# Seven block products in place of eight in parts of eight weight units of a decoder layer

## The chip, the cores and the metric

The kernel runs on one core of one Trainium2 chip. The metric is the device time of one execution in microseconds (us). The core has five engines that work in parallel, each through its own instructions in order: PE (TensorE, matrix products into the PSUM banks), DVE (VectorE), ACT (ScalarE), POOL (GpSimd) and SP (SyncE), which here only issues DMA transfers. POOL issues transfers too.

## The reference

One layer of a decoder trunk on 256 rows of 4096 columns, in float32:

```
u = RMSNorm(h)
one combined projection of u -> branch A (gated recurrence), branch B (differential attention),
                                two sigmoid gates of 4096 columns each
h = h + (sigmoid(g_A) * y_A + sigmoid(g_B) * y_B) @ wo      (y_A, y_B: the branches' outputs, projected)
out = RMSNorm(h)
```

The units that the change touches are plain products with large weights: the gates (u of 256 x 4096 by 4096 x 8192), and the output product (256 x 4096 by 4096 x 4096). The two branch projections (2048 x 4096 each) stand between them.

## The kernel before

**Weights.** All weights stream through one ring. SP loads pieces of 128 x 2048 float32 (1 MB, L104) into three buffers `w`. Each piece is split in two chunks of 1024 columns: ACT writes `hi` (L122), a copy rounded to the matrix engine's float32 format, and DVE writes `lo` = w - hi (L123). `hi` and `lo` have four buffers each, and the split runs up to three chunks ahead of PE (SPLIT_AHEAD). The activations are split in the same way into tiles `u`, `oh` and `y`, with a high and a low part.

**Products.** A product of one 128 x 128 block of activations with 512 columns of weights is three matmuls (L254, L255, L256): high by hi, high by lo, low by hi. One matmul takes 512 columns and accumulates in a PSUM bank of 128 x 512.

**Units.** After eight groups of branch work come eight gate units (`gate_unit`, `wide_unit`), each over 16 pieces: 1024 output columns as two blocks n by the 256 rows as two blocks t, so four banks. One piece holds two k-tiles (blocks of 128 of the inner dimension) by 1024 columns: eight block products, 24 matmuls. In the last piece the four banks are finished one after the other, ACT takes the sigmoid of each out of the bank with the rows' scale `rstd` (L310), and POOL stores it in DRAM (`g_dram`, L311). During gates 1 to 7 SP loads the branch outputs (`ol`), and ACT and DVE split them into `oh`. Then four branch units, each of two `wide_unit`s; DVE multiplies the banks with the gates read back (`gl`, L682, L686) and adds them (L687), PE transposes the result, and ACT and DVE split it into `y` (L696 and after). Last come eight output units of 512 columns (`mov_unit`, 8 pieces each): DVE adds x (`xr`, loaded through POOL) to the bank (L727), ACT squares with a running sum (L728), POOL multiplies with the norm's weight (L729). The last of them keeps six half-pieces (two of them in tiles of their own, `khi` and `klo`), so that the first 128 rows end early and their scaling and stores (`out_rows`, from L731) run beside the rest.

**Order.** The program is written out in Python in order of pieces (`run`); a scheduler turns it into one list per engine, in which loads and splits come before other work of the same time (priority AHEAD). Small work beside the stream is queued in `todo`, one entry after each piece. What an engine does in which order is then fixed.

Of the kernel before, what the change touches and what calls it, by code (L numbers as in the profile page):

```python
# [9 lines left out]
F32 = mybir.dt.float32  # L10
# [29 lines left out]
KEEP = 10  # L40
# [4 lines left out]
def trunk_kernel(ctx, tc, xT, x, nw, w_stat, w_mov, w_gate, w_branch, w_out, lbt, hnw, lamv, slw, fw, out):  # L45
# [8 lines left out]
    gp = ctx.enter_context(tc.tile_pool(name="gp", bufs=4))  # L54
    acc = ctx.enter_context(tc.tile_pool(name="acc", bufs=4, space=PSUM))
    mx = ctx.enter_context(tc.tile_pool(name="mx", bufs=4, space=PSUM))
# [26 lines left out]
    class Stream:  # L83
        def __init__(self):
            self.src = []
            self.raw = {}
            self.split = {}
            self.keep = {}
            self.loaded = 0
            self.done = 0  # L90

# [13 lines left out]

        def split_to(self, n):
            while self.done < min(n, 2 * len(self.src)):
                i = self.done
                self.load_to(i // 2 + 1)
                t = self.raw[i // 2]  # L110
                if i % 2:
                    del self.raw[i // 2]
                t = t[:, (i % 2) * HALF : (i % 2 + 1) * HALF]
                if i in self.keep:
                    hi, lo = self.keep.pop(i)
                else:
                    hi = whi.tile([P, HALF], F32R, name="hi", tag="hi")
                    lo = wlo.tile([P, HALF], F32R, name="lo", tag="lo")
                m = HALF // 2 if i < HEAD else HALF
                with tc.high_priority(AHEAD):  # L120
                    for c in range(0, HALF, m):
                        act.activation(hi[:, c : c + m], t[:, c : c + m], AF.Copy)  # L122
                        dve.tensor_tensor(lo[:, c : c + m], t[:, c : c + m], f32(hi[:, c : c + m]), op=ALU.subtract)  # L123
                self.split[i] = (hi, lo)
                self.done += 1

        def take(self, i):
            self.split_to(2 * i + SPLIT_AHEAD)
            yield self.split.pop(2 * i)
            self.split_to(2 * i + 1 + SPLIT_AHEAD)  # L130
            yield self.split.pop(2 * i + 1)
# [67 lines left out]
    def add(srcs, fn):  # L199

        for n, s in enumerate(srcs):
            stream.src.append(s)
            plan.append((n, fn))

    def run():
        for i in range(run.at, len(plan)):
            n, fn = plan[i]
            stream.load_to(i + LOAD_AHEAD)
            for r, (hi, lo) in enumerate(stream.take(i)):
                fn(2 * n + r, hi, lo)  # L210
            step()
        run.at = len(plan)
# [62 lines left out]
    def wide_unit(srcs, src_tiles, done):  # L275


        st = {}
        last = 2 * len(srcs) - 1

        def cols(r, n):
            c = n if r % 2 else 1 - n
            return slice(c * 512, (c + 1) * 512)

        def fn(r, hi, lo):
            if r == 0:
                st["ps"] = [[acc.tile([P, 512], F32, name="ps_w", tag="acc") for _ in range(2)] for _ in range(2)]
            ps = st["ps"]
            if r < last - 1:
                for n in range(2):  # L290
                    c = cols(r, n)
                    mov_mm([ps[t][n] for t in range(2)], src_tiles[r // 4], r % 4, hi[:, c], lo[:, c], r == 0, False)
                return
            st[r] = hi, lo
            if r < last:
                return
            for n in range(2):
                for t in range(2):
                    for k in (last - 1, last):
                        hi, lo = st[k]  # L300
                        c = cols(k, n)
                        mov_mm({t: ps[t][n]}, src_tiles[k // 4], k % 4, hi[:, c], lo[:, c], False, k == last, (t,))
                    done(t, n, ps[t][n])

        add(srcs, fn)

    def gate_unit(q):
        def done(t, n, ps):
            g = gp.tile([P, 512], F32, name="gt", tag="gt")
            act.activation(g, ps, AF.Sigmoid, scale=rstd[:, t : t + 1])  # L310
            pool.dma_start(g_dram[2 * q + n][t], g)  # L311

        wide_unit([w_gate[q, n] for n in range(16)], u, done)
# [39 lines left out]
    with tc.tile_pool(name="tmp", bufs=1) as tmp:  # L353
# [289 lines left out]
        gate_unit(0)  # L643
        run()
        while todo:
            step()

    with tc.tile_pool(name="op", bufs=1) as op:
        oh = [op.tile([P, 4, 2, S], F32R, name=f"oh{g}") for g in range(8)]

        def o_load(g, a):
            t = op.tile([P, 2, S], F32, name="ol", tag="gl", bufs=4)
            nc.sync.dma_start(t, o_dram[g][:, 2 * a : 2 * a + 2])
            return t

        def o_split(g, a, t):
            c = slice(2 * a, 2 * a + 2)
            act.activation(oh[g][:, c, 0, :], t, AF.Copy)
            dve.tensor_tensor(oh[g][:, c, 1, :], t, f32(oh[g][:, c, 0, :]), op=ALU.subtract)

        ol = {}
        for g in range(8):
            for a in range(2):
                todo.extend([lambda i=(g, a): ol.update({i: o_load(*i)}), None, None, lambda i=(g, a): o_split(*i, ol.pop(i))])
        for q in range(1, 8):
            gate_unit(q)


        y = []

        def branch_unit(q):
            rows, g = {}, {}

            def g_load(br):
                for n in range(2):
                    for t in range(2):
                        gl = g[t, n] = op.tile([P, 512], F32, name="gl", tag="gl", bufs=4)
                        nc.sync.dma_start(gl, g_dram[8 * br + 2 * q + n][t])

            def a_done(t, n, ps):  # L680
                r = rows[t, n] = gp.tile([P, 512], F32, name="yr", tag="gt")
                dve.tensor_tensor(r, ps, g[t, n], op=ALU.mult)  # L682

            def b_done(t, n, ps):
                r, gl = rows[t, n], g[t, n]
                dve.tensor_tensor(gl, ps, gl, op=ALU.mult)  # L686
                dve.tensor_tensor(r, r, gl, op=ALU.add)  # L687
                todo.append(lambda: turn(t, n))

            def turn(t, n):  # L690
                if t == 0:
                    y.append(uy.tile([P, 4, 2, S], F32R, name="y", tag="uy"))
                yt = y[2 * q + n]
                ps = mx.tile([P, 4, P], F32, name="ps_y", tag="mx")
                for j in range(4):
                    pe.transpose(ps[:, j], rows[t, n][:, j * P : (j + 1) * P], ident)  # L696
                c = slice(t * P, (t + 1) * P)
                act.activation(yt[:, :, 0, c], ps, AF.Copy)
# [156 lines left out]
```

## Time and profile before

| what | value |
|---|---|
| device time, median of 3 runs | 2894.07 us (2893.0 to 2894.49) |
| the profiled execution | 2894.51 us, its span 2892.5 us |
| granted TensorE clock, mean | 0.999 of full speed |
| PE busy | 2878.5 us (100%), 13782 instructions |
| DVE busy | 1478.8 us (51%) |
| ACT busy | 1326.0 us (46%) |
| POOL busy | 97.4 us (3%) |
| moved by DMA | 583.15 MB, 202 GB/s |

The span runs from the first to the last instruction of the profiled execution. The matmuls are pipelined: the duration of one contains part of the next, so that their spacing is read from their starts. Busy shares are averages over stages, and an idle engine that nobody waits for costs nothing.

### The profile page before, as it was taken

What the parts mean: (1) busy time and instruction counts of PE and PEld (TensorE: products, weight loads), DVE (VectorE), ACT (ScalarE), POOL (GpSimd) and SP (SyncE); (2) the same over time, 40 slices, a digit from 0 to 9 for tenths busy, and PEclk for the clock granted to TensorE, in tenths of its full rate; (3) what the DMA queues carried; (4) which work ended last, traced back from release to release, by engine and by line L of the source; (5) the groups of instructions that cost most, each with busy time, mean ns of one, the idle gap of its engine ahead of it and who ended that gap; (6) DMA issues with size and microseconds to landing.
All of it is one profiled execution on the core that took longest, in us unless ns stands there. A gap on an engine that the chain in (4) does not pass through costs nothing.

```text
span 2892.5 us, 33800 instructions
## 1 busy us (share of the span) xinstructions
PE 2878.5 (100%) x13782; PEld 2412.5 (83%) x13782; DVE 1478.8 (51%) x1497; ACT 1326.0 (46%) x1507; POOL 97.4 (3%) x113
## 2 busy tenths in 40 slices
PE   9999999999999999999999999999999999999998
PEld 8888888888888888888888888888888888888886
DVE  6546455454555554545545444444444555554444
ACT  7545454454444444444445434444434443344443
POOL 0000000000000000000000000000000000001010
PEclk9999999999999999999999999999999999999999
DMA  8555555555545555555557555556556556566564
GB/s 334 190 177 195 189 182 181 183 197 189 183 178 187 197 182 190 177 190 193 181 190 276 206 198 207 204 206 212 203 193 222 215 205 219 207 220 220 201 212 173
DMA packets 91804, 583.15 MB, mean 202 GB/s; under 512 B 10992, under 2 KB 11264, under 8 KB 26624
## 3 DMA queue, kind: packets, MB, share of 16 engines
q1 hardware_dynamic: 86112, 562.09, 54.9%
q0 software_dynamic: 5536, 18.89, 1.7%
q8 instruction: 108, 1.77, 0.2%
q14 instruction: 48, 0.39, 0.0%
HBM read 564.17 MB, written 16.78 MB: 201 GB/s over the span
## 4 chain that ended last, share of the span: by engine, by line
PE 95%; issue 3%; DMA 1%; ACT 0%; DVE 0%; SPq 0%; POOL 0%; DVEq 0%; ACTq 0%; POOLq 0%
PE ps_s L183 12%; PE ps_m L254 12%; PE ps_m L255 12%; PE ps_m L256 12%; PE ps_w L254 11%; PE ps_w L255 11%; PE ps_w L256 11%; PE ps_s L184 6%; PE ps_k L183 4%; PE ps_k L184 2%; DMA ol<-o_dram 1%; PE ps_sc L477 0%; PE ps_s L566 0%; PE ps_o L492 0%; PE ps_y L696 0%
## 5 line engine op out<-in xcount | busy, mean ns | idle before, releaser
L123 DVE TENSOR_TENSOR lo<-w,hi 128x1024 fp32r<-128x1024 f32 (+1 forms) x1026 | 1265.0, 1236 | 1345.1 <-ACT hi L122 1344.4
L122 ACT ACTIVATE hi<-w 128x1024 fp32r<-128x1024 f32 (+1 forms) x1026 | 1080.7, 1056 | 1473.4 <-PE ps_w L256 582.1
L183 PE MATMUL ps_s<-u,hi 128*128 128x512 f32 x1536 | 540.2, 396 | 0.0
L184 PE MATMUL ps_s<-u,lo 128*128 128x256 f32 x1536 | 431.7, 281 | 0.0
L254 PE MATMUL ps_m<-hi,u 128*128 128x512 f32 x1024 | 402.1, 393 | 0.0
L255 PE MATMUL ps_w<-lo,u 128*128 128x512 f32 x1024 | 399.0, 390 | 0.8 <-DVE lo L123 0.8
L254 PE MATMUL ps_w<-hi,u 128*128 128x512 f32 x1024 | 399.6, 390 | 0.0
L256 PE MATMUL ps_m<-hi,u 128*128 128x512 f32 x1024 | 398.7, 389 | 0.0
L255 PE MATMUL ps_m<-lo,u 128*128 128x512 f32 x1024 | 398.7, 389 | 0.0
L256 PE MATMUL ps_w<-hi,u 128*128 128x512 f32 x1024 | 398.4, 389 | 0.0
L183 PEld LDWEIGHTS ps_s<-u,hi 128*128 128x128 f32 x1536 | 288.0, 188 | 67.8 <-DVE half L190 0.2
L184 PEld LDWEIGHTS ps_s<-u,lo 128*128 128x128 f32 x1536 | 290.1, 189 | 0.3
L254 PEld LDWEIGHTS ps_w<-hi,u 128*128 128x128 f32 x1024 | 192.2, 188 | 42.7 <-ACT gt L310 2.6
L255 PEld LDWEIGHTS ps_w<-lo,u 128*128 128x128 f32 x1024 | 192.2, 188 | 40.7 <-DVE lo L123 1.1
L256 PEld LDWEIGHTS ps_m<-hi,u 128*128 128x128 f32 x1024 | 192.2, 188 | 40.3
L256 PEld LDWEIGHTS ps_w<-hi,u 128*128 128x128 f32 x1024 | 192.2, 188 | 39.9
L254 PEld LDWEIGHTS ps_m<-hi,u 128*128 128x128 f32 x1024 | 192.3, 188 | 39.5
L255 PEld LDWEIGHTS ps_m<-lo,u 128*128 128x128 f32 x1024 | 192.3, 188 | 39.1
L254 PE MATMUL ps_w<-hi,oh 128*128 128x512 f32 x512 | 200.6, 392 | 0.0
L256 PE MATMUL ps_w<-hi,oh 128*128 128x512 f32 x512 | 199.4, 389 | 0.0
L255 PE MATMUL ps_w<-lo,oh 128*128 128x512 f32 x512 | 199.3, 389 | 0.0
L254 PE MATMUL ps_m<-hi,y 128*128 128x512 f32 x504 | 196.5, 390 | 0.0
(182 smaller groups left out, 2254.9 us busy)
## 6 DMA issues: line engine op xcount, KB each, us to landing
w<-in_w_mov SPq DMA_DIRECT2D x156, 1024.0 KB, 4.8
w<-in_w_gate SPq DMA_DIRECT2D x128, 1024.0 KB, 4.8
w<-in_w_stat SPq DMA_DIRECT2D x96, 1024.0 KB, 4.8
w<-in_w_branch SPq DMA_DIRECT2D x64, 1024.0 KB, 4.8
w<-in_w_out SPq DMA_DIRECT2D x64, 1024.0 KB, 4.8
g_dram<-gt POOLq DMA_DIRECT2D x32, 256.0 KB, 5.9
gl<-g_dram SPq DMA_DIRECT2D x32, 256.0 KB, 4.5
o_dram<-oT POOLq DMA_DIRECT2D x8, 512.0 KB, 6.9
```

Source lines behind the costliest of these rows:

```text
L122: act.activation(hi[:, c : c + m], t[:, c : c + m], AF.Copy)
L123: dve.tensor_tensor(lo[:, c : c + m], t[:, c : c + m], f32(hi[:, c : c + m]), op=ALU.subtract)
L183: pe.matmul(ps, wh, ut[:, k].rearrange("p a s -> p (a s)"), start=first, stop=False)
L184: pe.matmul(ps[:, :S], wl, ut[:, k, 0, :], start=False, stop=last)
L254: pe.matmul(ps[t], uh, wh, start=first, stop=False)
L255: pe.matmul(ps[t], uh, wl, start=False, stop=False)
L256: pe.matmul(ps[t], ul, wh, start=False, stop=last)
```

## The change

A piece holds a 2 x 2 block matrix of weights (two k-tiles by two blocks of 512 columns), and the rows and k-tiles of the activations make a 2 x 2 block matrix too. Their product is eight block products as written, and seven by Strassen's method (in Winograd's form), with sums of blocks formed before and after. In five gate units (2 to 6) eight of the 16 pieces, and in three of four output units seven of 16, are now computed by the seven products ("S"); the other pieces stay as they are ("P"), and S and P alternate. Around this:

- For an S piece DVE forms three sums of weight blocks (L132 to L134; one in place, two blocks and one more in a tile `wt` with one buffer), and ACT and DVE split 3.5 chunks instead of 2 (four entries in the stream). `hi` and `lo` now have seven buffers each from gate 1 on, and the split runs up to five chunks ahead.
- The sums of activation blocks (`sf`, four blocks of 128 x 128 per piece) are formed once: for u during gate 1, for y during branch 3 and output unit 0. Before that u is multiplied with `rstd` in place during gate 0 (`norm`), so that the sigmoid needs no scale.
- A mixed unit has eight banks: four products of sums (P1, p5, P6, P7) and four blocks. At its end they are combined (`evict`): two ACT copies, four DVE operations, and one DVE addition per block (L423 in the gate units, L960 in the output units) ahead of the sigmoid or the addition of x. The two PSUM pools of before are closed after gate 0, and one pool of eight named banks takes their place.
- The output units are now four of 1024 columns (the weights are laid out accordingly), the last one with its last three pieces held. h goes to DRAM through POOL and comes back before the end; the multiplication with the norm's weight moves from POOL to DVE. `xr` is loaded by SP, half of the rows at a time. y goes through DRAM as well, stored and loaded through POOL. The loads and splits of the branch outputs move to gate 7.

```diff
+        def sums(self, i):
+            w = self.raw[i]
+            t = self.raw[i, "T"] = self.tp.tile([P, 1536], F32, name="wt", tag="wt")
+            dve.tensor_tensor(w[:, 0:512], w[:, 0:512], w[:, 512:1024], op=ALU.add)
+            dve.tensor_tensor(t[:, 0:512], w[:, 0:512], w[:, 1536:2048], op=ALU.subtract)
+            dve.tensor_tensor(
+                t[:, 512:1536].rearrange("p (a c) -> p a c", a=2), w[:, 512:1536].rearrange("p (a c) -> p a c", a=2),
+                t[:, 0:512].unsqueeze(1).to_broadcast([P, 2, 512]), op=ALU.subtract,
+            )
...
+                    if self.kind[i] == "S" and c == 0:
+                        self.sums(i)
+                    t = self.raw[i] if c < 2 else self.raw[i, "T"]
+                    o = (c % 2) * HALF
+                    w = HALF if c < 3 else 512
...
+    ORDER = (("P1", "p5"), (0, 1), ("P6", "P7"), (2,))
...
+        def evict(b):
+            if b in (0, 1, 2, 3):
+                final(b // 2, b % 2, ps[b], sb.get(("c", b)))
+                return
+            t = sb[b] = gp.tile([P, 512], F32, name="ut", tag="gt")
+            if b == "P1":
+                act.activation(t, ps[b], AF.Copy)
+                sb["c", 0] = t
+            elif b == "p5":
+                act.activation(t, ps[b], AF.Copy)
+            elif b == "P6":
+                dve.tensor_tensor(t, ps[b], sb["P1"], op=ALU.add)
+            else:
+                dve.tensor_tensor(t, ps[b], sb["P6"], op=ALU.add)
+                sb["c", 2] = t
+                dve.tensor_tensor(sb["P6"], sb["p5"], sb["P6"], op=ALU.subtract)
+                sb["c", 1] = sb["P6"]
+                dve.tensor_tensor(sb["p5"], sb["p5"], t, op=ALU.subtract)
+                sb["c", 3] = sb["p5"]
...
+            else:
+                dve.tensor_tensor(g, ps, g, op=ALU.add)
+                act.activation(g, g, AF.Sigmoid)
             pool.dma_start(g_dram[2 * q + n][t], g)
...
+        def norm(n):
+            f = joined(n)
+            dve.tensor_tensor(f, f, rstd_bc.unsqueeze(1).to_broadcast([P, 2, S]), op=ALU.mult)
+            p_form(u[n // 2], 2 * (n % 2), f)
...
+    early.close()
...
+    whi2 = ctx.enter_context(tc.tile_pool(name="whi2", bufs=3))
+    wlo2 = ctx.enter_context(tc.tile_pool(name="wlo2", bufs=3))
...
+    stream.ring = [(whi, wlo)] * 4 + [(whi2, wlo2)] * 3
+    stream.ahead = 5
...
+    SPLIT = (0, 2, 4, 6, 8, 10, 12, 14)
...
+    gate_unit(1, PLAIN, None, bank, post=u_sums)
+    for q in range(2, 7):
+        gate_unit(q, mix(16, SPLIT), us, bank)
+    gate_unit(7, PLAIN, None, bank, post=o_next)
...
+    def y_load(n):
+        t = yl[n] = gp.tile([P, 2, S], F32, name="yl", tag="gt")
+        pool.dma_start(t, y_dram[n // 2][:, 2 * (n % 2) : 2 * (n % 2) + 2])
...
+            else:
+                dve.tensor_tensor(tile_, ps, tile_, op=ALU.add)
+                dve.tensor_tensor(tile_, tile_, xt, op=ALU.add)
+            act.activation(xt, tile_, AF.Square, accum_out=ssq[:, t, b : b + 1])
+            dve.tensor_tensor(tile_, tile_, fwt[n], op=ALU.mult)
...
+            if t == 0 and n == 1:
+                io_x(1)
```

Three places in the order of the instructions. The first is DVE within a gate unit of before; each row is one split, and the numbers tell the buffers apart:

```order
L123 TENSOR_TENSOR lo_12109<-w_12072,hi_12108 128x1024
L123 TENSOR_TENSOR lo_12125<-w_12072,hi_12124 128x1024
L123 TENSOR_TENSOR lo_12143<-w_12106,hi_12142 128x1024
L123 TENSOR_TENSOR lo_12159<-w_12106,hi_12158 128x1024
L123 TENSOR_TENSOR lo_12179<-w_12140,hi_12178 128x1024
```

And DVE within a mixed gate unit now (L153 is the split):

```order
L132 TENSOR_TENSOR w_13119<-w_13119 128x512
L153 TENSOR_TENSOR lo_13122<-w_13085,hi_13121 128x1024
L133 TENSOR_TENSOR wt_13143<-w_13119 128x512
L134 TENSOR_TENSOR wt_13143<-w_13119,wt_13143 128x1024
L153 TENSOR_TENSOR lo_13132<-w_13085,hi_13131 128x1024
L153 TENSOR_TENSOR lo_13142<-w_13119,hi_13141 128x1024
L153 TENSOR_TENSOR lo_13156<-w_13119,hi_13155 128x1024
L153 TENSOR_TENSOR lo_13165<-wt_13143,hi_13164 128x1024
L153 TENSOR_TENSOR lo_13181<-wt_13143,hi_13180 128x512
L132 TENSOR_TENSOR w_13196<-w_13196 128x512
```

A pair of pieces was four splits; it is now six splits and three sums, and both splits of the P piece (`w_13085`) stand behind the first sum of the S piece that follows it (`w_13119`), the second one behind all three sums.

The second place is DVE at the end of a mixed gate unit; before, no DVE work of the unit's end stood there, only splits as above. `ut` are the products of sums, `ps_w` the banks:

```order
L369 TENSOR_TENSOR ut_13233<-ps_w_12683,ut_13205 128x512
L153 TENSOR_TENSOR lo_13252<-wt_13224,hi_13251 128x1024
L371 TENSOR_TENSOR ut_13238<-ps_w_12687,ut_13233 128x512
L153 TENSOR_TENSOR lo_13256<-wt_13224,hi_13255 128x512
L373 TENSOR_TENSOR ut_13233<-ut_13210,ut_13233 128x512
L423 TENSOR_TENSOR ut_13205<-ps_w_12667,ut_13205 128x512
L375 TENSOR_TENSOR ut_13210<-ut_13210,ut_13238 128x512
L423 TENSOR_TENSOR ut_13233<-ps_w_12671,ut_13233 128x512
L423 TENSOR_TENSOR ut_13238<-ps_w_12695,ut_13238 128x512
L423 TENSOR_TENSOR ut_13210<-ps_w_12714,ut_13210 128x512
L153 TENSOR_TENSOR lo_13298<-w_13249,hi_13297 128x1024
L153 TENSOR_TENSOR lo_13310<-w_13249,hi_13309 128x1024
```

The splits of the next unit's first piece (`wt_13224`) stand ahead of the final additions, those of its second piece (`w_13249`) behind all four.

The third place is SP at the end of a mixed output unit; before, SP had only weight loads there (x went through POOL):

```order
L104 DMA w_18769<-in_w_out 128x2048
L104 DMA w_18803<-in_w_out 128x2048
L104 DMA w_18837<-in_w_out 128x2048
L104 DMA w_18871<-in_w_out 128x2048
L104 DMA w_18911<-in_w_out 128x2048
```

Now, with the two loads of x for the ending unit and the two for the next one's first rows:

```order
L120 DMA w_20382<-in_w_out 128x2048
L951 DMA xr_20306<-in_x 128x512
L951 DMA xr_20308<-in_x 128x512
L951 DMA xr_20772<-in_x 128x512
L951 DMA xr_20774<-in_x 128x512
L120 DMA w_20417<-in_w_out 128x2048
```

Four loads of x stand between two weight loads, and SP takes them in this order.

## Rows read from the trace of the kernel before

**Rows 1.** Page: busy us (share) and instructions; clock; chain; costliest DVE group (us, mean ns):

```profile
PE 2878.5 (100%) x13782; PEld 2412.5 (83%) x13782; DVE 1478.8 (51%) x1497; ACT 1326.0 (46%) x1507; POOL 97.4 (3%) x113
PEclk9999999999999999999999999999999999999999
PE 95%; issue 3%; DMA 1%; ACT 0%; DVE 0%; SPq 0%; POOL 0%; DVEq 0%; ACTq 0%; POOLq 0%
L123 DVE TENSOR_TENSOR lo<-w,hi 128x1024 fp32r<-128x1024 f32 (+1 forms) x1026 | 1265.0, 1236 | 1345.1 <-ACT hi L122 1344.4
```

**Rows 2.** Time line inside a gate unit: start, duration, engine, line [idle before <-releaser]:

```profile
1501.18 1.06 ACT L122 ACTIVATE hi<-w 128x1024 fp32r<-128x1024 f32 x1 [1.66 <-PE ps_w L256]
1501.20 0.39 PE L255 MATMUL ps_w<-lo,u 128*128 128x512 f32 x1
...
1501.43 0.39 PE L256 MATMUL ps_w<-hi,u 128*128 128x512 f32 x1
...
1502.27 1.23 DVE L123 TENSOR_TENSOR lo<-w,hi 128x1024 fp32r<-128x1024 f32 x1 [1.49 <-ACT hi L122]
...
1503.90 1.06 ACT L122 ACTIVATE hi<-w 128x1024 fp32r<-128x1024 f32 x1 [1.66 <-PE ps_w L256]
```

**Rows 3.** Window of a gate unit: engines' busy us (instructions), clock, DMA share, GB/s:

```profile
1650.00:1735.00 85.00, 85.00 (x375) 70.11 (x374) 37.93 (x32) 34.72 (x34) 2.16 (x4) 1.00 0.58 205
```

**Rows 4.** Waits of the whole span: us in total, times, longest us:

```profile
DVE lo L123 <- ACT hi L122: 1344.4, 920, 3.5
ACT hi L122 <- PE ps_w L256: 582.1, 346, 3.7
...
PEld ps_w L254 <- ACT gt L310: 3.0, 8, 0.4
...
PE ps_w L255 <- DVE lo L123: 0.8, 1, 0.8
```

**Rows 5.** Time line of POOL: the first store of two gate units that follow each other:

```profile
1650.04 0.54 POOL L311 DMA_DIRECT2D g_dram<-gt  x1 [81.45 <-ACT gt L310]
...
1737.35 0.54 POOL L311 DMA_DIRECT2D g_dram<-gt  x1 [81.47 <-ACT gt L310]
```

**Rows 6.** Time line of DVE with queued work; last, a group (busy, mean ns | idle before):

```profile
2177.34 2.36 DVE L123 TENSOR_TENSOR lo<-w,hi 128x1024 fp32r<-128x1024 f32 x2 [3.53 <-ACT hi L122]
...
2261.06 1.28 DVE L686 TENSOR_TENSOR gl<-ps_w,gl 128x512 f32<-128x512 f32 x2
2262.26 1.28 DVE L687 TENSOR_TENSOR yr<-yr,gl 128x512 f32<-128x512 f32 x2
...
L686 DVE TENSOR_TENSOR gl<-ps_w,gl 128x512 f32<-128x512 f32 x16 | 10.6, 685 | 0.5
```

**Rows 7.** DMA issues; landings of L104 in 1560:2200, in 5:60; GB/s slices of 2150:2200:

```profile
w<-in_w_gate SPq DMA_DIRECT2D x128, 1024.0 KB, 4.8
g_dram<-gt POOLq DMA_DIRECT2D x32, 256.0 KB, 5.9
...
DMA to landing us min/median/max: 4.6/4.8/7.8
...
DMA to landing us min/median/max: 5.2/8.4/9.8
...
GB/s 275 0 118 321 400 13 52 236 439 111 0 144 419 275 0 98 347 393 0 52 111 341 318 370 410 210 311 295 170 262 419 98 13 131 419 288 0 105 315 413
```

**Rows 8.** Time line of the end, from the last bank to the scaling of the rows:

```profile
2881.73 0.69 DVE L727 TENSOR_TENSOR hbuf<-ps_m,xr 128x512 f32<-128x512 f32 x1 [3.12 <-PE ps_m L256]
2882.46 0.63 ACT L728 ACTIVATE xr<-hbuf 128x512 f32<-128x512 f32 x1 [3.90 <-DVE hbuf L727]
...
2883.74 1.76 ACT L739 ACTIVATE hbuf<-hbuf,r_h 128x512 f32<-128x512 f32 x2 [0.23 <-DVE r_h L734]
```

**Rows 9.** Time line of PE in the last output unit, matmuls on the kept tiles:

```profile
2873.24 0.40 PE L254 MATMUL ps_m<-khi,y 128*128 128x512 f32 x1
2873.48 0.40 PE L255 MATMUL ps_m<-klo,y 128*128 128x512 f32 x1
```

More of the change, by code (lines that the diff above doesn't have):

```diff
@@ L39 @@
 HEAD = 4
-KEEP = 10
 AHEAD = 100
@@ L104, in load_part, with tiles @@
             nc.sync.dma_start(self.raw[i][:, c : c + n], self.src[i][:, c : c + n])
-        def split_to(self, n):
[L107 to L119, printed above, removed]
-                with tc.high_priority(AHEAD):
[L121 to L124, printed above, removed]
+        def tiles(self):
+            a, b = self.ring[self.at % len(self.ring)]
+            self.at += 1
+            hi = a.tile([P, HALF], F32R, name="hi", tag="hi")
+            lo = b.tile([P, HALF], F32R, name="lo", tag="lo")
+            return hi, lo
@@ L125, in split_to @@
                 self.done += 1
         def take(self, i):
[L128 to L131, printed above, removed]
+            for n in range(self.first[i], self.first[i] + (4 if self.kind[i] == "S" else 2)):
+                self.split_to(n + self.ahead)
+                yield self.split.pop(n)
     stream = Stream()
@@ L273, in mov_unit @@
         add(srcs, fn)
[L275 to L283, printed above, removed]
-        def fn(r, hi, lo):
[L286 to L292, printed above, removed]
+    ORDER = (("P1", "p5"), (0, 1), ("P6", "P7"), (2,))
@@ L293, in fn @@
                 return
-            st[r] = hi, lo
-            if r < last:
+            if n <= last - tail:
+                plain(n, c, hi, lo, [(0, 0), (0, 1), (1, 0), (1, 1)])
                 return
[L297 to L310, printed above, removed]
-            pool.dma_start(g_dram[2 * q + n][t], g)
-        wide_unit([w_gate[q, n] for n in range(16)], u, done)
+            held[r] = hi, lo
+            if n < last or c == 0:
+                return
+            for blocks in ([[(t, m)] for t in range(2) for m in range(2)] if tail == 1
+                           else [[(t, m) for m in range(2)] for t in range(2)]):
+                for (k, c2), w in held.items():
+                    plain(k, c2, *w, blocks)
@@ L646, in trunk_kernel @@
             step()
[L648 to L698, printed above, removed]
-                dve.tensor_tensor(yt[:, :, 1, c], ps, f32(yt[:, :, 0, c]), op=ALU.subtract)
-            todo.extend([lambda: g_load(0)] + [None] * 7 + [lambda: g_load(1)])
-            wide_unit([w_branch[0, q, n] for n in range(8)], oh[:4], a_done)
-            wide_unit([w_branch[1, q, n] for n in range(8)], oh[4:], b_done)
-        for q in range(4):
-            run()
-            branch_unit(q)
-        run()
@@ L797 @@
+    for q in range(4):
+        out_unit(q)
+    run()
 _OUT = (S, D)
```

346 lines of the change are left out of this document (266 added, 80 removed).

## The prediction

> **What bounds the kernel now.** I read the page first. TensorE (PE) is busy for 100% of the span, its clock stands at the upper of its two levels (2.4 GHz) in every slice, and the chain that ended last is 95% PE [rows 1]. A busy PE need not be PE at its peak, so next comes the time line inside a gate unit: from one matmul to the next of the same form is 0.227 us (1501.20 to 1501.43), although one is listed as 0.39 long, because they overlap. In the 2.72 us between two `hi` copies (1501.18 to 1503.90) lie twelve matmuls, all that one chunk of weights feeds; in the same stretch DVE works once for 1.23 us and idles 1.49, and ACT works 1.06 and idles 1.66 [rows 2]. The windows say the same of a whole unit: 375 matmuls in 85 us, or 0.2267 each, with DVE busy 37.93 and ACT 34.72 [rows 3]. Last the waits: DVE waits 1344 us for ACT, ACT 582 for PE (a chunk buffer to come free), but PE waits for a split once, for 0.8 us. The only other repeated stall of PE is at the start of a gate unit, 8 times up to 0.4 us [rows 4]. So PE's count of matmuls is the time, and a removed matmul is worth 0.2267 us as long as the splits, the weight loads and the evictions keep ahead.
>
> **What is removed.** Each of the 5 mixed gate units turns 8 pieces of 24 matmuls into 8 of 21, each of the 3 mixed output units 7: 61 pieces by 3 matmuls, 183 in all, every one 128x512. 183 x 0.2267 = **41.5 us**, all on the path. The period of a gate unit is 87.3 us (1650.04 to 1737.35) [rows 5]; it should become 87.3 - 24 x 0.2267 = 81.9. The stalls at unit starts mostly go, since a mixed unit opens with banks that were emptied long before: five to six of 0.38 us. With that and the few matmuls on kept halves that go: -1 us or a little more, I take **-1**.
>
> **What is added on DVE.** A Strassen piece (S) has three sums (L132 and L133 of 512 columns, L134 of 1024) and four splits (three of 1024, one of 512), where a plain piece (P) has two splits. One 128x1024 operation is listed as 1236 ns and one 128x512 as 685 [rows 1, 6], but queued operations overlap: two splits took 2.36 together, and two 512-wide products that began at 2261.06 made way for the next at 2262.26, 0.60 each [rows 6]. So 1.13 to 1.24 and 0.60 to 0.69. S costs 4 x 1.13 + 3 x 0.60 = 6.3 (long form 4 x 1.24 + 3 x 0.69 = 7.0), P 2.3 (2.5), a pair 8.6 (9.5). PE needs 24 + 21 = 45 matmuls x 0.2267 = 10.2 for the pair. A mixed gate unit adds 8 evictions on DVE, 4.8 us: 8 x 8.6 + 4.8 = 73.6 of 81.6 (90%); in the long form 81.5, 100%. I take the overlapped form, as DVE's queue will be full; the other end, 100%, costs no more than a few tenths per unit. ACT copies 5.5 chunks per pair, about 1.06 each, 5.8 of 10.2: covered.
>
> **What DVE's order adds.** DVE works strictly in order, and in the mixed units a weight load hangs in that order too. The load of S piece k+1 needs the buffer of the P piece before, whose last reader is the split after L134; that comes 4.8 us after L132 of piece k (0.60 + 1.13 + 0.60 + 1.13 + 1.13, and about 0.2 because L133 and L134 depend on each other). Then 0.3 to issue and 4.8 to land [rows 7] until L132 of piece k+1 may start. The loop is 9.9 us per pair against PE's 10.2: PE stays the bound, by 0.3. Would two loads in flight lengthen the landing? The load of the following P goes out some 2.3 us later, and in a busy slice the DMA engines move up to 439 GB/s, so that a megabyte flows for about 2.4 us of its 4.8 [rows 7]: the flows hardly meet. I take 4.8. The bounds are 4.6 and the 8.4 of the opening, where loads were queued on one another [rows 7]. Break-even is a lasting 5.1 us. The seven split buffers hold about 7.5 us of lead, so that one late load costs nothing.
>
> **Unit ends.** At the end of a mixed unit DVE must stand before the last four additions (L423, L960) until PE has closed the banks, and behind them are queued the splits of the next unit's second piece. The first piece is split already: 21 matmuls, 4.8 us, and the P piece's matmuls begin only after them. In a gate unit the P splits are finished with some 2.9 us to spare by the durations above. In an output unit x must be reloaded for the second half of the rows (two loads behind an ACT square, 4.8 us by the landings of [rows 7]), the additions L961 wait for it, a split waits behind them, and SP holds further x loads ahead of a weight load. There I count a spare of 0.65 to 1 us, so 0 to 3 us of PE idle at each of two such ends. Gate 0 hands over to gate 1 through a closing of the PSUM pools: PE waits for the last sigmoid, **+0.7** (0.69 by the 512-wide DVE row in [rows 6] as the nearest, nothing hides it). In gate 7, SP's loads of `ol` wait for a g_dram write (5.9 us [rows 7]) ahead of a weight load, 0 to 3. For all of these together I take **+2** with 0 to 9 as bounds.
>
> **The tail.** Before, the last bank is followed by an addition at 2881.73 (0.69), a square (0.63) and short steps to the scaling at 2883.74 [rows 8]. Now the last unit ends with two banks per half, so one more addition L960, L961 and multiplication by fw on DVE in that chain, and a small reduction: 2 to 4 steps of 0.60, some of them under the square. **+2.2**, bounds 1 to 4.
>
> **The sum** is made against the profiled execution, 2894.5 us (span 2892.5 and 2.0 around it), 0.4 over the median: 2894.5 - 41.5 - 1 + 0.7 + 2 + 2.2 = 2856.9, by the median 2856.5. I say **2857**. Bounds of the small terms: 2852 to 2866.
>
> A page's price for the removed matmul: the Trainium skill, "TensorE: Matmul & The Clock Gate", section "Wait — 56ns, not 53.3ns?", gives a start-to-start of columns by 2.4 GHz and 2.5 ns, 215.7 ns for 512 columns. The trace shows 227 [rows 2], so by the page the removed term would be 39.5 in place of 41.5; the measurement decides.
>
> **Rivals.** (a) *The loop of sums, splits and loads becomes the bound in part.* For: its 9.9 lies 3% under PE's 10.2, and every duration in it is a median of an uncrowded DVE and of loads that flew alone. Against: two loads hardly meet. At a lasting landing of 5.5 us the pair takes 10.6; 0.4 x 61 = 24 less some 10 that the lead of eight units absorbs, so 2857 + 14 = 2871; at 5.75, 2880. (b) *Slower than before: the same loop, altogether the bound.* One mechanism: the load of an S piece lands so late that L132 holds DVE, and the P splits behind it. It wipes out the gain at a pair of 10.88 us, the 48 matmuls of before, which is a landing of 5.8; at 6.5 a pair takes 11.6: 2857 + 61 x 1.4 - 10 = 2932, 2910 if half of the pairs are hit. For it speaks the opening, 8.4 us with loads queued on one another; against it 4.8 as the median at DMA busy 58% [rows 3, 7], to which the change adds a sixteenth. (c) *Matmuls from other buffers run slower.* The rows on the separately placed `khi` and `klo` start 0.235 apart, where those on `hi` and `lo` start 0.227 apart [rows 9]. Three of the seven split buffers are now placed apart. If their share, three sevenths of some 5,600 matmuls, runs at 0.235: 2400 x 0.008 = 19, 2876; if all of them, 2900, no change. Those rows follow upon a change of tile, so they may show a passing state. (d) *The loads and stores on the POOL queue (y, h) come late beside a busy DVE.* Each of 16 y loads holds ACT in order; at 1.5 us each (a DVE operation and a bit) that is up to 24, less the lead: 2870. The issue on POOL takes 0.54 in the gate stores with DVE half busy [rows 3, 5], which says nothing of a full DVE. The Trainium skill, "SBUF — State Buffer", section "SBUF: two separate sides", says that descriptors of such DMAs wait while DVE holds a port that it shares with GpSimd; by that rule the change moves y to the wrong queue, and no row of before shows such a stall. (e) *The change doesn't do what it says.* The instructions of the changed program hold 183 fewer 512-wide matmuls, so no.
>
> **How the numbers follow.** Forecast 0.60 (2852 to 2866); (a) 0.18 (2866 to 2884); (c) 0.07 (2866 to 2900); (d) 0.04; (b) 0.07 (2900 to 2932, of it 0.02 within a hair of no change); other losses, none over 40 us, 0.04. The range holds the forecast and most of (a), (c) and (d): 2850 to 2882, 0.85 by these cases; I leave the rest for what I may have missed. A measurement of this kernel tells a difference of about 0.2% (6 us) from no change: faster 0.90 (all of the forecast, (a) and (d), most of (c) and of the other losses), same 0.04 (from (b) 0.02, from (c) and the others 0.01 each), slower 0.06 (the rest of (b) and of the others).
>
> **What would show it.** Right: 81.9 us between the first gate stores of two mixed units; 0.227 between matmuls everywhere; the chain still PE; DVE busy near 75% over the mixed units with short idle stretches ended by weight loads at L132. Wrong: PE's weight loads waiting for `lo` or `hi` for more than 10 us in sum (a, b); weight landings over 5.1 us in mixed units (a, b); 0.235 in every third matmul group (c); ACT waiting for `yl` (d); PE idle of over 3 us at each output unit's start (unit ends).

## The result and the profile after

The changed kernel takes **2857.44 us** (median of 4 runs, 2854.89 to 2858.94) against 2894.28 for the kernel before on the same chip; the ratio is 0.9872, with a 95% interval of 0.9855 to 0.9889. The forecast was 2857. The profiled execution took 2858.94 us with a span of 2857.2, which is 35.3 less than before. First the page's busy shares, the clock and DVE's costliest group, as in [rows 1]:

```profile
PE 2838.4 (99%) x13599; PEld 2379.8 (83%) x13599; DVE 1818.1 (64%) x2015; ACT 1447.4 (51%) x1692; POOL 97.9 (3%) x136
PEclk9999999999999999999999999999999999999999
L153 DVE TENSOR_TENSOR lo<-w,hi 128x1024 fp32r<-128x1024 f32 (+1 forms) x1028 | 1257.5, 1230 | 952.1 <-ACT hi L152 947.5
```

13782 matmuls have become 13599, 183 fewer. DVE works 339 us more and is still idle for a third of the whole span. The page's chain of waits says nothing here: it was followed back only as far as 2741, some 4% of the span. What sets the pace is read from the gate units. POOL's time line (start, duration, engine, line, [idle before <-releaser]), the first store of mixed units that follow each other, answers to [rows 5]:

```profile
1735.40 0.54 POOL L425 DMA_DIRECT2D g_dram<-ut  x1 [79.08 <-ACT ut L424]
...
1817.00 0.54 POOL L425 DMA_DIRECT2D g_dram<-ut  x1 [77.92 <-ACT ut L424]
...
1898.60 0.54 POOL L425 DMA_DIRECT2D g_dram<-ut  x1 [77.93 <-ACT ut L424]
```

81.60 us from unit to unit, where it was 87.3. That is 360 matmuls by 0.2267 (81.6): PE alone, without any addition. The window of most of one such unit (busy us of PE, PEld, DVE, ACT, POOL with instructions; clock, DMA share, GB/s) answers to [rows 3]:

```profile
1740.00:1816.00 76.00, 76.00 (x337) 62.94 (x336) 70.36 (x74) 45.95 (x49) 0.00 (x0) 1.00 0.64 225
```

DVE is busy for 70.36 of 76 us, 93%. So the change has brought DVE within a few per cent of becoming the bound, and the gain hangs on that margin. DVE's time line over one pair of pieces shows how it is kept:

```profile
1782.63 0.68 DVE L132 TENSOR_TENSOR w<-w 128x512 f32<-128x512 f32 x1
1783.23 1.22 DVE L153 TENSOR_TENSOR lo<-w,hi 128x1024 fp32r<-128x1024 f32 x1
1784.37 0.68 DVE L133 TENSOR_TENSOR wt<-w 128x512 f32<-128x512 f32 x1
1785.09 1.22 DVE L134 TENSOR_TENSOR wt<-w,wt 128x1024 f32<-128x1024 f32 x1
1786.23 1.22 DVE L153 TENSOR_TENSOR lo<-w,hi 128x1024 fp32r<-128x1024 f32 x1
1788.36 2.60 DVE L153 TENSOR_TENSOR lo<-w,hi 128x1024 fp32r<-128x1024 f32 x2 [0.92 <-ACT hi L152]
1791.09 1.83 DVE L153 TENSOR_TENSOR lo<-wt,hi 128x1024 fp32r<-128x1024 f32 x2
1792.83 0.68 DVE L132 TENSOR_TENSOR w<-w 128x512 f32<-128x512 f32 x1
```

From L132 to L132 are 10.2 us, PE's time for 45 matmuls. The only idle time of DVE, 0.92, is ended by an ACT copy, and ACT in turn waits for PE to free a chunk buffer. The order of the two splits of the plain piece around the sums, and the starts 0.60 and 1.14 after one another, are those of the forecast; where an operation needs the one just ahead of it (L134 after L133) it is 0.72. The waits of the whole span (us in total, times, longest) answer to [rows 4]:

```profile
ACT hi L152 <- PE ps_w L340: 492.2, 385, 3.7
...
ACT y L443 <- DMA yl<-y_dram: 8.7, 7, 2.6
...
DVE w L132 <- DMA w<-in_w_out: 8.0, 3, 5.1
...
PEld ps_w L340 <- DVE lo L153: 4.0, 2, 3.8
...
PEld ps_w L340 <- issue: 2.3, 2, 2.1
```

PE waits for a split twice in the whole span, 4.0 us in sum, nearly all of it in one stall of the last output unit. The 0.4 us at the start of each gate unit are gone, and so is the one wait for a split of [rows 4]. There are two places where PE stands. One is the handover from gate 0 to gate 1. ACT's time line, then PE's:

```profile
1565.58 1.04 ACT L152 ACTIVATE hi<-w 128x1024 fp32r<-128x1024 f32 x1
1566.53 0.67 ACT L421 ACTIVATE gt<-ps_w,rstd 128x512 f32<-128x512 f32 x1
...
1567.30 0.47 PE L340 MATMUL ps_w<-hi,u 128*128 128x512 f32 x1 [1.74 <-issue]
```

The last sigmoid, with a weight copy of 1.04 us ahead of it on ACT, ends at 1567.20, and PE starts at 1567.30, 2.12 us after its last matmul of gate 0 began (0.23 would be seamless). The other is the stall at 2780, in the last output unit (SP, POOL, DVE and PE on the time line):

```profile
2756.89 7.88 SPq L951 DMA_DIRECT2D xr<-in_x  x4
2764.86 12.35 SPq L120 DMA_DIRECT2D w<-in_w_out  x4
2767.85 0.54 POOL L992 DMA_DIRECT2D hb<-h_dram  x1
2778.05 0.53 POOL L992 DMA_DIRECT2D hb<-h_dram  x1 [9.66 <-PE ps_w L340]
2782.23 0.69 DVE L132 TENSOR_TENSOR w<-w 128x512 f32<-128x512 f32 x1 [5.13 <-DMA w<-in_w_out]
2784.11 0.50 PE L340 MATMUL ps_w<-lo,sf 128*128 128x512 f32 x1 [3.41 <-DVE lo L153]
```

The landings of the weight loads issued from 2760 to 2786:

```profile
DMA to landing us min/median/max: 6.1/10.1/10.4
```

And the window behind the stall (clock 0.57, DMA share 0.38, in the columns ahead of the GB/s):

```profile
2785.00:2789.00 4.00, 4.00 (x12) 3.11 (x11) 4.00 (x5) 0.10 (x1) 0.00 (x0) 0.57 0.38 117
```

For 8 us SP's queue holds loads of x, each behind an ACT square. Then weight loads and two reloads of h (`hb`, 1 MB each) are in flight together, the weight loads land after 10 us instead of 4.8, L132 waits 5.1 for one, and PE waits behind it; from matmul to matmul are 3.80 us, 3.57 of them idle. Behind the stall the granted clock is at its lower level (1.2 GHz) for a while: eight matmuls start 0.427 us apart in place of 0.227, another 1.6 us. The end, as in [rows 8]:

```profile
2844.35 1.37 DVE L960 TENSOR_TENSOR ut<-ps_w,ut 128x512 f32<-128x512 f32 x2 [1.17 <-PE ps_w L340]
2845.63 1.28 DVE L961 TENSOR_TENSOR ut<-ut,xr 128x512 f32<-128x512 f32 x2
2846.40 0.63 ACT L962 ACTIVATE xr<-ut 128x512 f32<-128x512 f32 x1 [3.26 <-DVE ut L961]
...
2849.08 0.72 ACT L932 ACTIVATE ut<-ut,r_h 128x512 f32<-128x512 f32 x1 [0.23 <-DVE r_h L927]
```

The last matmul begins at 2844.60, the span ends 12.6 us later; before it was 11.2 (2881.31 to 2892.5).

### The profile page after: what moved, and what is told of

Its sections match the earlier page's. It is cut to its first block, busy times and chain, and to the rows that moved or that the text cites. A ratio compares the mean times of both kernels' runs of the same rounds, so it can differ in the third digit from the quotient of the medians.

```text
span 2857.2 us, 34383 instructions
## 1 busy us (share of the span) xinstructions
PE 2838.4 (99%) x13599; PEld 2379.8 (83%) x13599; DVE 1818.1 (64%) x2015; ACT 1447.4 (51%) x1692; POOL 97.9 (3%) x136
## 5 line engine op out<-in xcount | busy, mean ns | idle before, releaser
L153 DVE TENSOR_TENSOR lo<-w,hi 128x1024 fp32r<-128x1024 f32 (+1 forms) x1028 | 1257.5, 1230 | 952.1 <-ACT hi L152 947.5
L340 PE MATMUL ps_w<-hi,u 128*128 128x512 f32 x1648 | 521.3, 389 | 1.7 <-issue 1.7
L340 PEld LDWEIGHTS ps_w<-hi,u 128*128 128x128 f32 x1648 | 309.3, 188 | 66.4 <-issue 2.1
L340 PE MATMUL ps_w<-lo,u 128*128 128x512 f32 x824 | 321.0, 390 | 0.0
L340 PE MATMUL ps_w<-hi,oh 128*128 128x512 f32 x1024 | 318.8, 390 | 0.0
L340 PE MATMUL ps_w<-hi,y 128*128 128x512 f32 x814 | 259.7, 391 | 0.0
L340 PEld LDWEIGHTS ps_w<-hi,oh 128*128 128x128 f32 x1024 | 192.2, 188 | 39.9
L340 PEld LDWEIGHTS ps_w<-lo,u 128*128 128x128 f32 x824 | 154.7, 188 | 32.0
L215 PE MATMUL ps_k<-u,hi 128*128 128x512 f32 x512 | 181.0, 400 | 0.1
L340 PEld LDWEIGHTS ps_w<-hi,y 128*128 128x128 f32 x814 | 153.5, 189 | 32.1
```

Source lines behind the costliest of these rows:

```text
L153: dve.tensor_tensor(lo[:, k : k + m], t[:, o + k : o + k + m], f32(hi[:, k : k + m]), op=ALU.subtract)
L215: pe.matmul(ps, wh, ut[:, k].rearrange("p a s -> p (a s)"), start=first, stop=False)
L340: pe.matmul(ps[b], a, w, start=first, stop=left[b] == 0)
```

## The experiments

The first four ask what the gain is made of and how near DVE is to being the bound, the other eight what the stall at 2780 comes from.

### All pieces plain

```diff
-        gate_unit(q, mix(16, SPLIT), us, bank)
+        gate_unit(q, PLAIN, us, bank)
...
-        kinds = PLAIN if q == 0 else mix(16, Y_SPLIT)
+        kinds = PLAIN
```

> The changed kernel with every piece plain again (eight products in the five gate units and the three output units); the ring of seven buffers, the closing of the pools, y and h through DRAM and the wide output units stay. Theory (a matmul is worth 0.2267 us, the sums cost PE nothing but the one stall seen in the last output unit): 183 matmuls come back, 41.5 us, and the stall with its slow matmuls, 5.2 us, goes: 2857 + 41.5 - 5 = 2894, gate periods 87.1 us, PE without a gap over 1 us from gate 2 on to the tail. Rival (the sums hold PE up all along, in pieces too small to see): under 2885. Rival (the rest of the change costs more than the gate 0 handover of 1.9 and the tail of 2): over 2900.

Measured: 2894.39 us, ratio to the kernel before 1.0001 (0.9991 to 1.0010). The first stores of its gate units:

```profile
1738.78 0.54 POOL L425 DMA_DIRECT2D g_dram<-gt  x1 [82.16 <-ACT gt L421]
...
1825.82 0.54 POOL L425 DMA_DIRECT2D g_dram<-gt  x1 [82.16 <-ACT gt L421]
```

87.04 us per unit, 384 x 0.2267, and no gap of PE over 1 us from gate 2 to the tail. Everything else that the change moves (y and h through DRAM, wide output units, seven buffers, the closing of the pools) comes out at nothing in sum, and the seven products alone bring 2894.4 - 2857.4 = 37.0 us: the 41.5 of 183 matmuls, less the stall and its slow matmuls, which this kernel doesn't have. The gate units' starts are seamless here too, although each unit takes the same four banks again. So the 0.4 us of [rows 4] goes without the banks of mixed units, which the forecast gave as its reason; what took it away isn't shown.

### PE made faster: what is the next bound?

```diff
-            for a, w in ((uh, wh), (uh, wl), (ul, wh)):
+            for a, w in ((uh, wh), (uh, wl), (ul, wh))[: 2 if two else 3]:
```

with `two` in gate units 2 to 6.

> The changed kernel with the third matmul of each product (low part of u by hi) left out in gate units 2 to 6, so that PE needs 240 x 0.2267 = 54.4 us for a unit and something else must set its period. The scheduler moves the splits of a plain piece ahead of the sums of the next here. Theory (DVE's own work is the next bound, operations overlapped, 0.60 and 1.13): 75 to 77 us from unit to unit, the time 2857 - 5 x 6 = 2827. Rival (DVE operations at their full listed length): 81 us, 2855. Rival (the loop of load and splits, 9.9 per pair, is there in any order): 80 to 84, 2850 to 2865.

Measured: 2819.03 us in one run. POOL's stores at the ends of three units:

```profile
1801.35 2.33 POOL L425 DMA_DIRECT2D g_dram<-ut  x4 [70.36 <-ACT ut L424]
1876.21 2.33 POOL L425 DMA_DIRECT2D g_dram<-ut  x4 [72.53 <-ACT ut L424]
1951.18 2.33 POOL L425 DMA_DIRECT2D g_dram<-ut  x4 [72.63 <-ACT ut L424]
```

And the window of most of one unit:

```profile
1740.00:1800.00 60.00, 50.37 (x191) 35.09 (x190) 59.74 (x65) 38.17 (x44) 0.00 (x0) 0.95 0.65 232
```

74.9 us per unit, with DVE busy for 59.74 of 60. So DVE is the next bound, at 74.9 where the sum of its operations, overlapped, gave 73.6 and their full length 81.5. PE's 81.6 stands 6.7 us above that, 8%. (The total is 8 us below the expected 2827: the unit's period had been taken as 75.6, and the five units together, from the last store of gate 1 to that of gate 6, took 371 us, where the changed kernel took 410.) The loop of load and splits with the order of the changed kernel isn't tested by this run: the scheduler put the plain splits ahead of the sums.

### Eleven of 16 pieces by seven products

```diff
+    MORE = [n for n in range(16) if n % 3 < 2]
...
-        gate_unit(q, mix(16, SPLIT), us, bank)
+        gate_unit(q, mix(16, MORE), us, bank)
```

> The changed kernel with eleven of 16 pieces by Strassen in gate units 2 to 6 (two S, one P), the activation sums of a neighbouring piece standing in where none were formed, which leaves the result of those pieces wrong but all work in place. PE needs 351 x 0.2267 = 79.6 us per unit, DVE 11 x 6.3 + 5 x 2.3 + 4.8 = 85.6. Theory (DVE overlapped is the next bound): a period of 86 to 88 us, in all 2857 + 5 x 5 = 2882, PE waiting for lo. Rival (PE is the bound still, DVE has more room than counted): 79.6, 2847. Rival (full listed length of DVE's operations): 95, 2924.

Measured: 2879.16 us in one run.

```profile
1821.56 0.54 POOL L425 DMA_DIRECT2D g_dram<-ut  x1 [77.89 <-ACT ut L424]
...
1908.65 0.54 POOL L425 DMA_DIRECT2D g_dram<-ut  x1 [77.50 <-ACT ut L424]
```

The period is 87.1 (the next one 89.1), a little over DVE's 85.6, though PE has 9 matmuls fewer per unit than in the changed kernel. The window of most of one unit shows PE idle for 3.7 of 80 us and DVE for only 1.3:

```profile
1745.00:1825.00 80.00, 76.26 (x331) 61.24 (x329) 78.74 (x88) 45.84 (x52) 0.54 (x1) 1.00 0.59 215
```

PE was expected to wait for `lo`; it waits more for `hi` (its weight loads 17.4 us against 5.8, from 1740 to 2000), as ACT's copies in turn wait for DVE's sums. Past the balance each further Strassen piece costs DVE 4 us and gives PE back 0.68.

### One pool of banks from the start

```diff
-    early.close()
-    psb = ctx.enter_context(tc.tile_pool(name="psb", bufs=1, space=PSUM))
```

with `psb` opened at the start, and `acc` and `mx` taking four of its banks each in turn.

> The changed kernel with one pool of eight named PSUM banks from the start, so that no pool is closed between gate 0 and gate 1. Theory (the gap of 2.1 us at 1565 is the wait for the last sigmoid before the pools may close): the gap falls to 0.3 to 0.6 us, the time by 1.6 to 1.8. Rival (the gap is the sum of other waits there, splits that come late or the rewritten u): the gap stays over 1.5 us.

Measured: 2855.01 us in one run. Gate 1 now begins without a stop, 0.23 after the last matmul of gate 0, and only its ninth matmul waits for the last sigmoid. The weight load of that one:

```profile
1567.36 0.19 PEld L348 LDWEIGHTS ps_w<-hi,u 128*128 128x128 f32 x1 [0.24 <-ACT gt L429]
```

The largest gap there is 0.32 from matmul to matmul, in place of 2.12: eight matmuls (1.8 us) on banks that are free already run beside the last copy and the last sigmoid. The stall at 2780 is there as before (2.86), so it is the closing that cost 1.8.

### Later reloads of h, twice without effect

```diff
-                if n in (2, 4, 6):
-                    i = n // 2 - 1
+                if n in (5, 8, 11):
+                    i = n // 3 - 1
```

> The changed kernel with the three reloads of h (1 MB each, through POOL) after pieces 5, 8 and 11 of the last output unit instead of 2, 4 and 6. Theory (the stall at 2780 comes from two reloads that share the DMA engines with weight loads, so that these land after 10 us instead of 4.8): the gap of 3.8 us falls under 0.6, the slow matmuls behind it go too, 2857.4 - 5.2 = 2852; weight loads in the first half of the unit land in 5 to 6 us. Rival (the x loads that hold SP's queue ahead of a weight load from 2757 to 2765 are enough): a gap of 2 us or more stays.

Measured: 2858.62 us, but POOL issues the reloads where it did:

```profile
2770.10 0.54 POOL L992 DMA_DIRECT2D hb<-h_dram  x1 [0.75 <-PE ps_w L340]
2780.30 0.53 POOL L992 DMA_DIRECT2D hb<-h_dram  x1 [9.66 <-PE ps_w L340]
2793.30 0.53 POOL L992 DMA_DIRECT2D hb<-h_dram  x1 [12.47 <-PE ps_w L340]
```

POOL has no other work there, and each load goes out when its buffer comes free (each row's wait ends at PE), wherever the program has it. A gap of 2.89 stayed, and nothing follows on its cause. The same held for the attempt to give the reloads other buffers, by three tiles of the ring that are taken and left unused:

> The changed kernel with the three reloads of h moved for good: they go into the buffers of y's fourth to sixth tile, which PE reads in pieces 6 to 11 of the last output unit, so that they can't be issued before some 2795. (The run that only wrote them later in the program left them at 2770, 2780 and 2793, since the scheduler issued them as soon as their buffers were free.) Theory (the stall at 2780 comes from the reloads on the DMA engines together with the weight loads): gap of PE there under 0.6 us, weight loads between 2765 and 2790 land in 5 to 6 us; time 2852 if the handover of gate 0 stays as it is. Rival (the x loads and the splits behind them are enough, the reloads only add): a gap of 1 to 2 us stays.

2856.68 us, reloads at 2765, 2775 and 2791, a gap of 3.14 and slow matmuls behind it.

### x through POOL

```diff
-                nc.sync.dma_start(xr[t, m], x[t * P : (t + 1) * P, b * 512 : (b + 1) * 512])
+                pool.dma_start(xr[t, m], x[t * P : (t + 1) * P, b * 512 : (b + 1) * 512])
```

> The changed kernel with the loads of x in the output units issued by POOL instead of SP, so that no weight load is queued behind them; h is reloaded as early as in the changed kernel. Theory (either of the two, SP's queue or the reloads of h, takes about half of the lead, and both together stall PE): the weight load of 2764.9 goes out some 7 us earlier and the gap falls under 1 us, time 2852 to 2853. Rival (the reloads alone are enough): gap over 2 us, time over 2855.

Measured: 2859.55 us; the gap at 2780 is 4.80, no smaller, and a new one of 1.84 stands at the end of output unit 0, where x now comes too late. The theory that freeing SP's queue is enough falls. The first weight load of the last output unit didn't go out 7 us earlier: it is issued 6.99 us after the unit's first matmul, where it was 7.67. The split that frees its buffer stands on DVE behind an addition that still waits for x:

```profile
2761.37 1.34 DVE L961 TENSOR_TENSOR ut<-ut,xr 128x512 f32<-128x512 f32 x2 [1.45 <-DMA xr<-in_x]
```

So this run doesn't show what an early weight load would do.

> As the run with x through POOL, and the second half of x has a buffer of its own, so that its load needs no square of the first half and the additions L961 of a unit's end find it there. Theory (the wait of DVE for x, 2.0 us in sum in the changed kernel, matters only through the lead): no gap over 0.5 us at the three unit ends, time 2851 to 2853, and no row of DVE waiting for xr. Rival (reloads of h alone are enough): a gap of over 2 us stays.

With a buffer of its own for the second half (in the place of a tile of sums that is free by then): 2857.81 us, no gap at the first two ends, 2.20 at the last. One run each, so the difference between 2.2 and 3.8 may be chance in part; but the stall is there without any x load in SP's queue and without a wait for x.

### The reloads tied to later pieces

```diff
+                    act.activation(hb[i][:, 0:1], f32(stream.split[max(stream.split)][1])[:, 0:1], AF.Copy)
                     pool.dma_start(hb[i], h_dram[i].rearrange("p t n c -> p (t n c)"))
```

with `n in (4, 7, 10)`; the ACT copy writes one column that the reload overwrites, and needs a late split.

> The changed kernel with each reload of h tied to the split of a later piece (one ACT copy of a single column into the reload's tile ahead of it; the two runs before left the reloads where they were, at 2765 to 2793, as their buffers were still free early), so that they go out at about 2790, 2805 and 2822. Theory (the stall at 2780 needs the reloads beside the weight loads): gap there under 0.6 us, weight loads between 2765 and 2788 land in 5 to 6 us, at most 1 us of PE idle where the reloads are now; total 2852 to 2854. Rival (x loads in SP's queue are enough): a gap of 1 to 3 us stays at 2780.

Measured: 2854.12 us in one run, beside 2891.92 for the kernel before, so that the time by itself shows little. POOL's reloads:

```profile
2789.64 0.53 POOL L993 DMA_DIRECT2D hb<-h_dram  x1 [22.14 <-ACT hb L992]
2799.05 0.53 POOL L993 DMA_DIRECT2D hb<-h_dram  x1 [8.87 <-ACT hb L992]
```

The landings of the weight loads issued from 2760 to 2786:

```profile
DMA to landing us min/median/max: 4.7/6.0/8.7
```

The gap is gone (0.34, with SP's x loads where they were), the landings are 6.0 at the median against 10.1, and the clock stays at its upper level. So the stall needs the reloads beside the weight loads; that is shown. The reloads alone don't make it: in the run with eleven of 16 pieces they go out at the same time within the unit and the weight loads land after 8 to 11 us, yet PE has no gap there (DVE's order at that unit's end is another one). What the x loads add can be read from the runs with x on SP and the same order of DVE there. The time from the first of the four x loads to the weight load behind them varies, and the gap with it. SP's rows in the run with the faster PE, where it is shortest:

```profile
2720.66 5.96 SPq L951 DMA_DIRECT2D xr<-in_x  x4
2726.73 0.38 SPq L120 DMA_DIRECT2D w<-in_w_out  x1
```

| run | first x load to weight load, us | gap of PE, us |
|---|---|---|
| PE made faster | 6.07 | 1.69 |
| one pool of banks | 7.21 | 2.86 |
| reloads written later | 7.25 | 2.89 |
| reloads in other buffers | 7.70 | 3.14 |
| changed kernel | 7.97 | 3.80 |
| reloads tied to later pieces | 7.25 | 0.34 |

With the reloads beside them, 1.9 us by which the weight load goes out later lengthen the gap by 2.1; without the reloads the same delay costs next to nothing. So x sets the size of the stall, as far as single profiles of kernels that differ elsewhere can show it. With x on POOL and in buffers of its own the gap was 1.8 to 2.2 in three runs.

### All mends together

> One pool of PSUM banks from the start, h reloaded later, x through POOL with a buffer of its own: all three mends together. Theory: 2857.4 - 5.2 (stall and slow matmuls of the last unit) - 1.8 (handover of gate 0) = 2850, no gap of PE over 0.6 us from gate 0 to the tail, ratio to the kernel before 0.985. Rival (another unit end takes over, or POOL's queue delays x): 2853 or more.

With the reloads "late" but not tied: 2851.42 us, ratio 0.9861 (0.9845 to 0.9878), a gap of 2.00 at 2776. With the reloads in other buffers, which moved nothing:

> The run with all mends, with h reloaded into the buffers that come free late. Theory: no gap of PE over 0.6 us from gate 0 to the tail; 2851.4 - 1.8 = 2849.5, ratio to the kernel before 0.985. Rival (the stall moves to the places where the reloads are now): 2851 or more.

2851.08 us, a gap of 1.82. And with the reloads tied:

> The run with all mends, with the reloads of h tied to later pieces. Theory: no gap of PE over 0.6 us from gate 0 to the tail, 2851 - 1.8 = 2849.5. Rival (the reloads stall PE wherever they are, since the lead of an output unit stays small): 2851 or more, with a gap of 1 us or more between 2790 and 2840.

2849.77 us (2849.26 to 2850.14, 4 runs), ratio 0.9853 (0.9836 to 0.9869). No gap remains in the output units; at the handover one of 1.04 came up in the profiled run, PE's row first. A weight load came late there, and the sigmoids stood behind the copy that waited for it:

```profile
1565.56 0.50 PE L348 MATMUL ps_w<-hi,u 128*128 128x512 f32 x1 [0.66 <-ACT gt L429]
1562.35 1.06 ACT L160 ACTIVATE hi<-w 128x1024 fp32r<-128x1024 f32 x1 [0.72 <-DMA w<-in_w_gate]
```

This version has the lowest median: 0.19% of the time of before, or 5.5 us, below the changed kernel by the two ratios, whose intervals overlap. (The kernel before took 2891.92 beside it, 2.4 less than beside the changed kernel, so that the times themselves aren't compared.)

Part of the difference between two executions comes from no edit. Ahead of gate 0 stand the same 7554 matmuls in every kernel here, and yet gate 0's first matmul begins at 1474.59 in the profile of the changed kernel and at 1472.14 in this one (from 1471.6 to 1475.0 in the fourteen profiles). Of the 9.0 us between these two executions 2.4 lie there; from gate 0 to the last matmul the mends bring 6.5.

## Why the prediction was right, and where not

**The removed matmuls: right.** 183 x 0.2267 = 41.5, and 81.60 us per mixed unit. The forecast of 81.9 had kept a stall at the units' starts that went.

**What DVE adds: right, at the overlapped end.** The faster PE gave 74.9 per unit for DVE, against 73.6 forecast from starts 0.60 and 1.13 apart and 81.5 from the listed durations. The choice of the starts in [rows 6] over the mean durations of [rows 1, 6] decided that. The Trainium skill, "Vector Engine (DVE) Microarchitecture Reference", section "5.2 Measured stream behaviour on trn2 (trn3 not measured)", gives 1.0417 ns per column and some 75 ns per instruction once they overlap in the queue, by which I estimate 1.14 and 0.61; the trace agrees, with 1.14 and 0.60. In the list of signs I wrote that DVE would be busy near 75% in mixed units; it is 93%, and my own sum said 90%. That sign was wrong by carelessness, not by theory.

**The loop through SP: right so far as it was met, with the issue counted twice.** The P piece's second split ends at 1787.45 and the next L132 begins at 1792.83, 5.4 us later. SP's row of the load between them, and its landing:

```profile
1787.47 0.33 SPq L120 DMA_DIRECT2D w<-in_w_gate  x1
DMA to landing us min/median/max: 4.8/4.8/4.8
```

The landing counts from the start of the issue, so that the 0.3 for the issue is part of the 4.8. The loop is 9.6 us and not 9.9, the spare 0.6 per pair and not 0.3, and break-even a lasting landing of 5.4. DVE waits only 1.0 us in all of the mixed gate units for a weight load. What a lasting longer landing does over many units wasn't tried; where it happened once, at 2780, PE stood.

**Unit ends: the right place, half of the cause, and too small.** I had put 0 to 3 us at each of two output units' ends, from x loads in SP's queue. One end cost 3.6 us of idle PE and 1.6 of slow clock, 5.2 in all, against +2 taken. The delay by x was there as forecast, but by itself it cost next to nothing (0.34 from matmul to matmul with the reloads tied). It took the reloads of h beside the weight loads, which the forecast's terms didn't contain at all: rival (d) names h beside y, but prices y alone, and only as coming late itself. The other ends, and gate 7 with its `ol` loads, cost nothing.

**The handover: mis-sized.** 0.7 was the one sigmoid that PE would wait for; 1.9 was measured (2.12 less the 0.23 of a seamless start), as a weight copy of 1.04 us stands ahead of that sigmoid on ACT. The wait was right, the queue in front of the releaser was forgotten.

**Stalls that go, the tail.** Eight unit starts by 0.23 and a wait of 1.1 for a split in gate 0, together 2.9 against the 1 taken; the reason given (banks emptied long before) isn't needed, as the plain run shows. The tail grew by 1.4 (12.6 less 11.2) against 2.2.

In sum the small terms are 1.9 + 5.2 + 1.4 - 2.9 = 5.6 in the profiled run, where 3.9 were forecast. That gives 2894.5 - 41.5 + 5.6 = 2858.6, and 2858.9 was measured. (Gate 0 also began 1.0 us later than in the profile of before, 1474.59 against 1473.60, ahead of anything that the change touches; so the account closes within a microsecond, not better.) That the median fell on 2857 owes something to the two errors of opposite sign.

**The rivals.** (a) and (b) stay possible mechanisms whose point wasn't reached: the weight loads of the gate units land in 4.8 us at the median as before. (By its own terms (a) comes to 2887 at a landing of 5.75 and not to 2880: 0.65 x 61 - 10 = 30.) (c) is refuted: matmuls from the three buffers placed apart keep 0.2267, since the unit's 360 take 81.60 together. The 0.235 of [rows 9] recurs in the trace of after for single matmuls behind the stalls and at the first pieces of the branch units and of output unit 0, 0.009 each, and nowhere in the mixed gate units. (d): ACT waits 8.7 us for y in seven places and PE never for that; the issue on POOL stays at 0.54 with DVE at 93%. The rule of the Trainium skill, "SBUF — State Buffer", section "SBUF: two separate sides", that such descriptors wait while DVE runs an operation in a two-port mode, has a condition that the forecast left out. No run here shows whether it was met, or separates this rule from other reasons for late loads of y; in the time nothing came of it.

## What to carry to other kernels

Price an engine that is about to become busy by starts of queued operations, not by listed durations: here the two differ by 7.9 us of a unit's 81.6, more than the whole margin of 6.7. When work is traded from the bound engine to one in the middle, measure the new margin by speeding the bound engine up (leave out some of its work) or by trading more, rather than by busy shares. When the lead is short, count every transfer that flies beside the weight loads: the delay by x cost next to nothing alone, and 5.2 us with the reloads beside it. A load written later in the program wasn't issued later here; a dependence on late data moved it.

## What was not expected of the hardware

After 3.57 us without a matmul (2780) the granted clock was at its lower level for eight matmuls, 1.6 us in sum; after 2.63 (the same place in the run with one pool) it stayed at the upper one, and after 2.5 at the handover it fell in the run with x in buffers of its own, whose window reads 0.57:

```profile
1568.00:1572.00 4.00, 4.00 (x11) 3.17 (x12) 3.64 (x6) 0.77 (x1) 0.54 (x1) 0.57 0.90 322
```

So the length of the idle time alone doesn't tell whether the clock falls. What it cost on top of a stall of 2 to 4 us went from nothing to as much again: in the run with the reloads in other buffers, 14 matmuls behind 2.9 us of idle time took 3.0 us more. That this makes the changed kernel's runs spread over 4 us, where the version without the stalls spreads over 0.9, isn't shown, since one execution of each was profiled; the time before gate 0, which no edit touches, differs by up to 3.4 us between the profiles.
